# LayerNorm ahead of the MLP: every second eviction of its transposes moved from ScalarE to VectorE

## The chip, the cores and the metric

The kernel runs on one NeuronCore of a Trainium2 chip. The metric is device time in microseconds (us) of one execution; lower is better. A core has TensorE for matmuls and transposes (in the profile PE, its weight loads PEld), VectorE (DVE), ScalarE (ACT), GpSimd (POOL) and SyncE (SP); each works through its own list of instructions in order. TensorE writes only to PSUM, in banks of 128 partitions by 512 float32; VectorE and ScalarE read results from there ("evict" them) into SBUF.

## The reference

A decoder trunk of two layers, in float32, on 1024 tokens of width 1024. Each layer is a token mixer of four head groups, an output projection with a residual and a LayerNorm, and an MLP with a squared ReLU, again with a residual and a LayerNorm:

```python
mix = jnp.concatenate([y_a, y_b, y_c, y_d], axis=-1) @ w_out[l]
h = layer_norm(DEEPNORM_ALPHA * h + mix, ln1_g[l], ln1_b[l])
ff = jnp.square(jax.nn.relu(h @ w_up[l])) @ w_down[l]
h = layer_norm(DEEPNORM_ALPHA * h + ff, ln2_g[l], ln2_b[l])
```

`layer_norm` subtracts the mean of a row, divides by the standard deviation, multiplies by g and adds b. `w_up` is 1024 by 4096 and `w_down` 4096 by 1024.

## The kernel before

**Matmuls.** Every float32 matmul is made of three with operands split in a high and a low part (`mm3`, lines 247 to 249, and `mm3_on`, line 256). Splitting costs a copy on ScalarE (the high part) and a subtraction on VectorE (the low part): for weights in `split_w` (lines 217 and 218), for activations in `to_act` (lines 210 and 211), for the MLP's hidden values in `prep` (lines 1186 and 996).

**The stage around the change.** The output projection adds its results to eight token tiles `z` of 128 tokens by 1024 (line 954: VectorE adds a PSUM bank `pg`). After every second tile, `ln_stats` (lines 139 to 150) gives mean and reciprocal deviation of two tiles, ScalarE writes the normalised tiles `zu` (line 962), and `to_act` turns them into the MLP's operand with channels on partitions. For a pair of token tiles it takes the 8 blocks of 128 channels two at a time, `j` = 0 and 1: one PSUM tile `pt` of 512 columns holds both, each filled by two transposes (line 202). A block is then evicted with g and b of its channels as scale and offset (line 207 on ScalarE, or line 204 on VectorE), into the float32 tile `f`, which is kept for the MLP (`keep`); two blocks together are split into `mh` (ScalarE, line 210) and `ml` (VectorE, line 211). Per layer that is 4 pairs of 4 `pt` tiles, so 64 transposes, 32 evictions and 16 splits. Only this call of `to_act` passes `keep`; the calls for the first LayerNorm and for the last one of a layer do not. `pt` has two buffers (`NPT`), `zu` shares the 13 buffers of `z`, where three are left for it.

VectorE also turns each `z` into the residual for the MLP (lines 1307 and 1308), 1024 columns at a time, once the tile's `zu` exists. TensorE goes on with the first quarter of the MLP's first product (`up_plain`; `pg` from `mh`, `ml` and the split weights `wuh`, `wul`), which ScalarE evicts with ReLU and square (lines 1019 and 1020). From the second quarter on the MLP runs as a Strassen product with 7 in place of 8 block products (`up_steps`, `down_steps`). It needs sums of the quarters of the activations: `sums_of_input` (line 1030) makes them from the `f` tiles on VectorE (`f` by lines 996 and 999), splits them (`sx`, lines 1038 on ScalarE and 996 on VectorE) and has GpSimd write them to DRAM (`sd`, line 1041), from where `fetch` reads them later (`s`, line 1055). Meanwhile the first `down_steps` prepares its operands (`sa`, `wd`) on the same two engines.

**What sets the order.** The program is recorded in the order of the Python code and then put in order for each engine by a scheduler that simulates a time line (`schedule_with_timeline_sim=True`), with `boost()` raising the priority of some pieces. At run time each engine keeps that order and waits where an operand is not there. In the names below the pairs of token tiles have these `pt` tiles in the first layer: pt_5571, 5582, 5591, 5602 (first pair), 5684, 5693, 5702, 5711 (second), 5793, 5804, 5813, 5824 (third), 5906, 5915, 5924, 5933 (fourth); f00 and f01 (f_5254, f_5255) belong to the first four token tiles, f10 and f11 to the others, and so do the `mh` and `ml` of these numbers.

Of the kernel before, what the change touches and what calls it, by code (L numbers as in the profile page):

```python
# [44 lines left out]
def trunk_kernel(ctx, tc, x, ln_in_g, ln_in_b, w_in, conv_w, conv_b, rg_wa, rg_ba, rg_wx, rg_bx, rg_lambda,  # L45
# [29 lines left out]
    def t_u(dt, shape, nm):  # L75
        return big.tile(shape, dt, tag="u", name=nm, bufs=4)

    def t_m(shape, nm):
        return mid.tile(shape, F32, tag="m", name=nm, bufs=NM)
# [10 lines left out]
    def p_t():  # L90
        return pm.tile([P, 512], F32, tag="t", name="pt", bufs=NPT)
# [95 lines left out]
    def to_act(act, zs, nt, gcol, bcol, keep=None):  # L187


        half, o, n = nt // 4, (nt % 4) * P, len(zs)  # L190
        kn = 4 // n
        for g in range(KT // kn):
            pt = p_t().rearrange("p (k c) -> p k c", k=kn)
            k0 = kn * g
            if keep is None:
                h32 = t_m([P, kn, n * P], "h32")
            else:
                h32 = keep[half][k0 // 4][:, k0 % 4:k0 % 4 + kn, o:o + n * P]
            for j in range(kn):
                k = k0 + j  # L200
                for i in range(n):
                    T.transpose(pt[:, j, i * P:(i + 1) * P], zs[i][:, k * P:(k + 1) * P], ident)
                if n == 1 and j % 2:
                    V.tensor_scalar(out=h32[:, j, :], in0=pt[:, j, :], scalar1=gcol[:, k:k + 1],
                                    scalar2=bcol[:, k:k + 1], op0=ALU.mult, op1=ALU.add)
                else:
                    A.activation(h32[:, j, :], pt[:, j, :], AF.Identity, scale=gcol[:, k:k + 1], bias=bcol[:, k:k + 1])
            hi, lo = act.alloc(half, k0 // 4)
            hs, ls = [t[:, k0 % 4:k0 % 4 + kn, o:o + n * P] for t in (hi, lo)]
            A.activation(hs, h32, AF.Copy)  # L210
            V.tensor_tensor(out=ls, in0=h32, in1=hs.bitcast(F32), op=ALU.subtract)
# [633 lines left out]
    for n0, n1 in FIRST:  # L845
        zp = zs[n0:n1]
        ln_unit(zp)
        to_act(act, zp, n0, *ln_in)
        for i in range(n0, n1):
            nc.sync.dma_start(out=spill[i], in_=zs[i])  # L850
        if n0 >= AHEAD:
            next(first, None)
# [19 lines left out]
    for l in range(DEPTH):  # L872
# [72 lines left out]
        keep = [[t_u(F32, [P, 4, 512], f"f{h}{g}") for g in range(2)] for h in range(2)]  # L945
        wo.append(load_out(1))
        for n in range(2):
            for nt in range(NT):
                t = slice((nt % 4) * P, (nt % 4) * P + P)
                ps = p_g()  # L950
                mm3(ps, [((ya.get(0, 2 * j + k, nt // 4)[:, t], ya.get(1, 2 * j + k, nt // 4)[:, t]),
                          (wo[n][j][0][k], wo[n][j][1][k])) for j in KOUT for k in range(2)])
                zc = zs[nt][:, 512 * n:512 * n + 512]
                V.tensor_tensor(out=zc, in0=zc, in1=ps, op=ALU.add)  # L954
                if n == 1 and nt % 2:
                    pair = slice(nt - 1, nt + 1)
                    mean, r = ln_stats(zs[pair], mv[:, pair, :], rs[:, pair])
                    nb = t_s([P, 2], "lnnb")
                    V.scalar_tensor_tensor(out=nb, in0=mean, scalar=-1.0, in1=r, op0=ALU.mult, op1=ALU.mult)
                    zu = [t_z([P, DM], "zu") for _ in range(2)]  # L960
                    for i in range(2):
                        A.activation(zu[i], zs[nt - 1 + i], AF.Identity, scale=r[:, i:i + 1], bias=nb[:, i:i + 1])
                    to_act(act, zu, nt - 1, *[c[:, 8 * l:8 * l + 8] for c in ln1], keep)
# [305 lines left out]
        def last_down(c, us):  # L1269
# [15 lines left out]
            for nt in range(NT):  # L1285
                t = slice(nt * P, nt * P + P)
                for n in range(2):
                    ps = p_g()
                    o = slice(n * 512, n * 512 + 512)
                    mm3(ps, [((us[i][0][:, f, t], us[i][1][:, f, t]), (ws[2 * i + f][0][:, o], ws[2 * i + f][1][:, o]))  # L1290
                             for i in range(2) for f in range(2)])
                    zc = zs[nt][:, o]
                    with boost() if nxt is None and nt == NT - 1 else nullcontext():
                        V.tensor_tensor(out=zc, in0=zc, in1=ps, op=ALU.add)
                if nxt is None:
                    with boost() if nt == NT - 1 else nullcontext():
                        ln_full(zs[nt], gb, bb, out[0, nt * P:(nt + 1) * P, :], nt == NT - 1)
                elif nt % 2:
                    zp = zs[nt - 1:nt + 1]
                    ln_unit(zp)  # L1300
                    to_act(nxt, zp, nt - 1, *[c[:, 8 * l:8 * l + 8] for c in ln2])
                    for i in range(2):
                        nc.sync.dma_start(out=spill[nt - 1 + i], in_=zp[i])
# [95 lines left out]
```

## Time and profile before

| | |
|---|---|
| runs shown | 2425.48, 2427.72, 2433.21 us; median 2427.72 us |
| the profiled execution | 2428.56 us, its span 2426.8 us |
| TensorE busy | 2362.7 us, 97% of the span |
| VectorE busy | 1759.9 us, 73% |
| ScalarE busy | 1115.3 us, 46% |
| granted TensorE clock, mean | 0.994 |
| mean DMA rate | 99 GB/s |

Shares of the whole span say little about a stage. The views used below are the windows (busy time of each engine in a stretch, with the granted TensorE clock), the list of who waited for whom, the groups of like instructions with their mean duration, and the time line of one engine, where a bracket at a row's end gives the idle time before it and what ended that. Matmuls are pipelined: the duration of one is longer than the distance to the next.

### The profile page before, as it was taken

The numbers are of one execution on the slowest core, as the hardware profiler recorded it, in microseconds if no ns is written. First come the engines' busy times: TensorE is split into PE (matmuls) and PEld (weight loads), VectorE is DVE, ScalarE is ACT, GpSimd is POOL, SyncE is SP. The second block draws the span as 40 slices with busy tenths as digits, with TensorE's granted clock in tenths as the row PEclk, the third lists the DMA queues.
The fourth block names the chain that finished last, engine by engine and source line by source line (L and its number), as shares of the span: only waits on it lengthen the run. The fifth ranks groups of instructions, "written<-read, shape, count | busy, mean of one in ns | idle before, by whom it ended". The sixth has DMA issues, their size and how long they took to land.

```text
span 2426.8 us, 35032 instructions
## 1 busy us (share of the span) xinstructions
PE 2362.7 (97%) x13924; PEld 1966.9 (81%) x13924; DVE 1759.9 (73%) x3088; ACT 1115.3 (46%) x1737; POOL 99.4 (4%) x180
## 2 busy tenths in 40 slices
PE   7999999999899999999999999999998999999997
PEld 6888888877788888888798887888777888888886
DVE  6467785766977787777745758856669777787778
ACT  6424655526444345444462346482264444345441
POOL 0000011000100000000000000300001000000000
PEclk9999999999999999999999999999999999999999
DMA  5211133220833224322221011512126433224322
GB/s 198 58 36 45 36 111 111 87 87 18 312 122 111 98 87 139 122 90 95 85 86 46 28 36 40 194 57 87 53 85 244 139 122 106 102 87 139 122 70 87
DMA packets 126971, 241.31 MB, mean 99 GB/s; under 512 B 8924, under 2 KB 81240, under 8 KB 118616
## 3 DMA queue, kind: packets, MB, share of 16 engines
q1 hardware_dynamic: 106032, 135.55, 17.1%
q0 software_dynamic: 19648, 102.80, 11.7%
q8 instruction: 110, 1.80, 0.3%
q10 hardware_dynamic: 1128, 0.72, 0.1%
q14 instruction: 53, 0.43, 0.1%
HBM read 201.29 MB, written 37.75 MB: 99 GB/s over the span
## 4 chain that ended last, share of the span: by engine, by line
PE 67%; issue 21%; DVE 8%; ACT 1%; DMA 1%; POOL 1%; DVEq 0%; POOLq 0%; ACTq 0%
PE pg L256 19%; PE pt L256 11%; PE pg L248 7%; PE pg L247 7%; PE pg L249 7%; PE ps L256 5%; PE po L256 3%; PE po L600 2%; PE pt L592 2%; DVE wdl L218 2%; DVE z L999 1%; PE ps L407 1%; DVE wd L996 1%; PE ps L413 1%; DVE s L999 1%
## 5 line engine op out<-in xcount | busy, mean ns | idle before, releaser
L218 DVE TENSOR_TENSOR wul<-wu,wuh 128x1024 fp32r<-128x1024 f32 x106 | 129.4, 1220 | 130.9 <-PE pg L256 55.1
L256 PE MATMUL pg<-wdh,sa 128*128 128x512 f32 x560 | 184.9, 396 | 6.0 <-DVE z L999 6.0
L217 ACT ACTIVATE wuh<-wu 128x1024 fp32r<-128x1024 f32 x106 | 111.8, 1056 | 123.3 <-PE po L256 54.5
L218 DVE TENSOR_TENSOR wdl<-wd,wdh 128x1024 fp32r<-128x1024 f32 x96 | 117.0, 1219 | 43.8 <-ACT wdh L217 26.9
L256 PE MATMUL pt<-s,wuh 128*128 128x512 f32 x448 | 137.9, 389 | 0.0
L256 PE MATMUL pg<-s,wuh 128*128 128x512 f32 x448 | 137.9, 389 | 0.0
L256 PEld LDWEIGHTS pg<-wdh,sa 128*128 128x128 f32 x560 | 107.1, 191 | 30.2 <-DVE z L999 6.9
L256 PE MATMUL pt<-wdh,sa 128*128 128x512 f32 x352 | 117.2, 393 | 7.0 <-DVE sa L996 4.5
L217 ACT ACTIVATE wdh<-wd 128x1024 fp32r<-128x1024 f32 x96 | 101.0, 1053 | 41.5 <-PE pg L256 12.8
L996 DVE TENSOR_TENSOR sa<-u,sa 128x512 fp32r<-128x512 f32 x140 | 91.4, 682 | 38.7 <-ACT sa L1186 38.7
L256 PE MATMUL ps<-wdh,sa 128*128 128x512 f32 x352 | 116.3, 390 | 0.0
L256 PE MATMUL pg<-mh,wuh 128*128 128x512 f32 x280 | 108.9, 389 | 0.0
L256 PE MATMUL pg<-ml,wuh 128*128 128x512 f32 x280 | 108.9, 389 | 0.0
L256 PE MATMUL pg<-wdl,sa 128*128 128x512 f32 x280 | 108.7, 396 | 0.0
L256 PE MATMUL pg<-mh,wul 128*128 128x512 f32 x280 | 108.6, 389 | 0.0
L247 PE MATMUL pg<-wo,yh 128*128 128x512 f32 x256 | 102.8, 402 | 3.1 <-DVE z L954 2.7
L248 PE MATMUL pg<-wo,yh 128*128 128x512 f32 x256 | 102.0, 398 | 0.0
L249 PE MATMUL pg<-wo,yl 128*128 128x512 f32 x256 | 99.9, 397 | 0.0
L256 PEld LDWEIGHTS pg<-s,wuh 128*128 128x128 f32 x448 | 84.1, 188 | 17.4
L256 PEld LDWEIGHTS pt<-s,wuh 128*128 128x128 f32 x448 | 84.1, 188 | 17.4
L1186 ACT ACTIVATE sa<-u 128x512 fp32r<-128x512 f32 x140 | 82.2, 623 | 22.7 <-PE ps L256 10.0
L999 DVE TENSOR_TENSOR z<-z,pg 128x512 f32<-128x512 f32 x140 | 90.2, 677 | 0.0
(411 smaller groups left out, 6872.0 us busy)
## 6 DMA issues: line engine op xcount, KB each, us to landing
s<-sd POOLq DMA_DIRECT2D x64, 1024.0 KB, 7.3
wu<-in_w_up_dram SPq DMA_DIRECT2D x64, 512.0 KB, 3.7
wd<-in_w_down_dram SPq DMA_DIRECT2D x64, 512.0 KB, 3.6
sd<-sx POOLq DMA_DIRECT2D x32, 512.0 KB, 7.9
spill<-z SPq DMA_DIRECT2D x16, 512.0 KB, 4.4
wb<-in_w_in_dram SPq DMA_DIRECT2D x16, 512.0 KB, 4.3
rs<-spill POOLq DMA_DIRECT2D x32, 256.0 KB, 5.9
resid<-rs POOLq DMA_DIRECT2D x32, 256.0 KB, 4.9
```

Of the source, the lines that this page charges most:

```text
L217: A.activation(hi, raw, AF.Copy)
L218: V.tensor_tensor(out=lo, in0=raw, in1=hi.bitcast(F32), op=ALU.subtract)
L247: T.matmul(ps, ah, bh, start=(i == 0), stop=False)
L248: T.matmul(ps, ah, bl, start=False, stop=False)
L249: T.matmul(ps, al, bh, start=False, stop=(i == n - 1))
L256: T.matmul(ps, a, b, start=(first and i == 0 and j == 0), stop=(i == n - 1 and j == 2), skip_group_check=not first)
L407: T.matmul(ps[r, c, :], k[r, cs], q[r, cs], start=True, stop=True)
L592: T.transpose(pt[:, j * P:(j + 1) * P], s[:, j * P:(j + 1) * P], ident)
L600: T.matmul(po[DH * par:DH * par + DH, (nb % 4) * P:(nb % 4 + 1) * P], vt[:, kb, e:e + DH], wts[par][:, j * P:(j + 1) * P], start=(diag and ...
L996: V.tensor_tensor(out=out, in0=x, in1=y, op=ALU.subtract)
L999: V.tensor_tensor(out=out, in0=x, in1=y, op=ALU.add)
L1186: A.activation(hi, src, AF.Copy)
```

## The change

The condition that chooses VectorE for the odd one of two blocks held only where one token tile is handled alone (`n == 1`); now it holds also where `keep` is given, that is in the LayerNorm ahead of the MLP, in both layers.

```diff
-                if n == 1 and j % 2:
+                if j % 2 and (n == 1 or keep is not None):
                     V.tensor_scalar(out=h32[:, j, :], in0=pt[:, j, :], scalar1=gcol[:, k:k + 1],
                                     scalar2=bcol[:, k:k + 1], op0=ALU.mult, op1=ALU.add)
                 else:
                     A.activation(h32[:, j, :], pt[:, j, :], AF.Identity, scale=gcol[:, k:k + 1], bias=bcol[:, k:k + 1])
```

Per layer 16 of 32 evictions move. The scheduler answers by another order on every engine, from the first pair's evictions to the first steps of `down_steps`; before and behind these stretches the order is the same. Three places in the first layer matter below; the second layer has the same order under other numbers.

**First place, VectorE, the second pair of token tiles.** Before, these rows stand between the last additions of the output projection:

```order
L218 TENSOR_TENSOR wul_6027<-wu_6024,wuh_6026 128x1024
L1308 SCALAR_TENSOR_TENSOR z_5240<-z_5240,rs_77,lnp_5250 128x1024
L218 TENSOR_TENSOR wul_6033<-wu_6030,wuh_6032 128x1024
L140 BN_AGGR mv_76<-lnst_5885 128x2
L954 TENSOR_TENSOR z_5246<-z_5246,pg_5859 128x512
L211 TENSOR_TENSOR ml00_5579<-f00_5254,mh00_5578 128x2x256 x2
```

Now:

```order
L218 TENSOR_TENSOR wul_6027<-wu_6024,wuh_6026 128x1024
L1308 SCALAR_TENSOR_TENSOR z_5240<-z_5240,rs_77,lnp_5250 128x1024
L218 TENSOR_TENSOR wul_6033<-wu_6030,wuh_6032 128x1024
L954 TENSOR_TENSOR z_5246<-z_5246,pg_5859 128x512
L140 BN_AGGR mv_76<-lnst_5885 128x2
L204 TENSOR_SCALAR f00_5254<-pt_5684,lnc1_850 128x256
L204 TENSOR_SCALAR f00_5254<-pt_5693,lnc1_850 128x256
L139 BN_STATS lnst_5885<-z_5246 128x6
L211 TENSOR_TENSOR ml00_5579<-f00_5254,mh00_5578 128x2x256
```

The evictions of pt_5684 and pt_5693 stand on VectorE behind the weight splits, the residual and the last addition.

**Second place, TensorE, between the third and the fourth pair.** Before:

```order
L202 MATMUL pt_5906<-ident_91,zu_5902 128x128
L247 MATMUL pg_6063<-mh01_5598,wuh_6032 128x512
L248 MATMUL pg_6063<-ml01_5599,wuh_6032 128x512
L249 MATMUL pg_6063<-mh01_5598,wul_6033 128x512
L247 MATMUL pg_6063<-mh01_5598,wuh_6032 128x512
L248 MATMUL pg_6063<-ml01_5599,wuh_6032 128x512
L249 MATMUL pg_6063<-mh01_5598,wul_6033 128x512
L247 MATMUL pg_6063<-mh01_5598,wuh_6032 128x512
L248 MATMUL pg_6063<-ml01_5599,wuh_6032 128x512
L249 MATMUL pg_6063<-mh01_5598,wul_6033 128x512
L202 MATMUL pt_5906<-ident_91,zu_5903 128x128
```

Now:

```order
L249 MATMUL pg_6063<-mh01_5598,wul_6033 128x512
L202 MATMUL pt_5813<-ident_91,zu_5789 128x128
L202 MATMUL pt_5813<-ident_91,zu_5790 128x128
L202 MATMUL pt_5824<-ident_91,zu_5789 128x128
L202 MATMUL pt_5824<-ident_91,zu_5790 128x128
L202 MATMUL pt_5906<-ident_91,zu_5902 128x128
L202 MATMUL pt_5915<-ident_91,zu_5902 128x128
L202 MATMUL pt_5906<-ident_91,zu_5903 128x128
L202 MATMUL pt_5915<-ident_91,zu_5903 128x128
```

The last transposes of the third pair and the first of the fourth stand back to back, 16 transposes in a row up to the next matmul, which reads mh10; no matmul is left between them.

**Third place, the end of the LayerNorm.** The first sum of the input (line 999) on VectorE, before and then now:

```order
L211 TENSOR_TENSOR ml10_5801<-f10_5256,mh10_5800 128x2x256 x2
L211 TENSOR_TENSOR ml11_5821<-f11_5257,mh11_5820 128x2x256
L999 TENSOR_TENSOR f11_5257<-f10_5256,f11_5257 128x1024
L996 TENSOR_TENSOR f10_5256<-f00_5254,f10_5256 128x1024
L996 TENSOR_TENSOR sx1_6216<-f11_5257,sx0_6215 128x1024
L211 TENSOR_TENSOR ml11_5821<-f11_5257,mh11_5820 128x2x256
```

```order
L211 TENSOR_TENSOR ml10_5801<-f10_5256,mh10_5800 128x2x256 x2
L204 TENSOR_SCALAR f11_5257<-pt_5924,lnc1_850 128x256
L204 TENSOR_SCALAR f11_5257<-pt_5933,lnc1_850 128x256
L211 TENSOR_TENSOR ml11_5821<-f11_5257,mh11_5820 128x2x256 x2
L999 TENSOR_TENSOR f11_5257<-f10_5256,f11_5257 128x1024 x2
```

The first sum stands behind the evictions of pt_5924 and pt_5933. Before, the second halves of their transposes were apart on TensorE: those of pt_5924 stood three matmuls behind the first halves, those of pt_5933 twenty-one. Now all stand twenty matmuls behind:

```order
L247 MATMUL pg_6144<-mh10_5800,wuh_6026 128x512
L248 MATMUL pg_6144<-ml10_5801,wuh_6026 128x512
L249 MATMUL pg_6144<-mh10_5800,wul_6027 128x512
L202 MATMUL pt_5924<-ident_91,zu_5902 128x128
L202 MATMUL pt_5924<-ident_91,zu_5903 128x128
L202 MATMUL pt_5933<-ident_91,zu_5902 128x128
L202 MATMUL pt_5933<-ident_91,zu_5903 128x128
```

On ScalarE the sums' high parts (sx0, line 1038) move behind evictions of the MLP's first product: before, four of them stand ahead of `u10_5954<-pg_6090` (line 1019), now one.

## Rows read from the trace of the kernel before

**Rows 1.** The page: busy times of each engine; the chain that ended last.

```profile
PE 2362.7 (97%) x13924; PEld 1966.9 (81%) x13924; DVE 1759.9 (73%) x3088; ACT 1115.3 (46%) x1737; POOL 99.4 (4%) x180
...
PE 67%; issue 21%; DVE 8%; ACT 1%; DMA 1%; POOL 1%; DVEq 0%; POOLq 0%; ACTq 0%
```

**Rows 2.** Windows: stretch, length, busy time of each engine (instructions), TensorE clock, DMA.

```profile
571.00:577.00 6.00, 4.32 (x22) 2.53 (x21) 6.00 (x9) 5.67 (x11) 0.00 (x0) 1.00 0.51 165
577.00:599.00 22.00, 22.00 (x106) 17.93 (x105) 10.54 (x19) 13.02 (x22) 0.00 (x0) 1.00 0.01 4
599.00:604.00 5.00, 3.53 (x19) 2.09 (x18) 1.91 (x3) 4.62 (x10) 0.00 (x0) 1.00 0.00 0
...
644.00:649.00 5.00, 5.00 (x15) 3.92 (x16) 5.00 (x7) 2.04 (x3) 0.66 (x2) 0.66 1.11 403
```

**Rows 3.** Waits of TensorE from 540 to 660: us in total, times, longest.

```profile
PE pt L256 <- DVE sa L996: 2.9, 1, 2.9
PE pt L202 <- ACT f L207: 2.3, 4, 0.8
PE pg L256 <- DVE z L999: 2.2, 1, 2.2
```

**Rows 4.** Groups by line and shape, whole run: count | busy us, mean ns | idle before.

```profile
L207 ACT ACTIVATE f<-pt,lnc 128x256 f32<-128x256 f32 x64 | 34.2, 565 | 34.7 <-PE pt L202 34.7
...
L954 DVE TENSOR_TENSOR z<-z,pg 128x512 f32<-128x512 f32 x32 | 21.7, 682 | 23.5 <-PE pg L249 23.1
```

**Rows 5.** The same groups, of VectorE alone: its small reads of PSUM.

```profile
L672 DVE TENSOR_TENSOR bsc<-ps,decay 128x256 f32<-128x256 f32 x32 | 12.7, 418 | 3.1 <-PE ps L671 2.9
...
L204 DVE TENSOR_SCALAR h<-pt,lnc 128x128 f32<-128x128 f32 x8 | 3.1, 398 | 0.0
```

**Rows 6.** Time line of VectorE around the second pair: start, length, instruction, idle before.

```profile
562.11 1.28 DVE L139 BATCH_NORM_STATS2 lnst<-z 128x6 f32<-128x512 f32 x2
564.58 1.28 DVE L1307 SCALAR_TENSOR_TENSOR z<-z,mv,lnp 128x1024 f32<-128x1024 f32 x1 [1.19 <-ACT zu L962]
...
574.71 1.29 DVE L211 TENSOR_TENSOR ml<-f,mh 128x512 fp32r<-128x512 f32 x2
```

**Rows 7.** Time line of TensorE around the second pair.

```profile
570.92 0.60 PE L202 MATMUL pt<-ident,zu 128*128 128x128 f32 x4
571.95 0.89 PE L202 MATMUL pt<-ident,zu 128*128 128x128 f32 x4 [0.44 <-ACT f L207]
```

**Rows 8.** Time line of ScalarE around the fourth pair.

```profile
595.70 1.25 ACT L962 ACTIVATE zu<-z,lnnb,rs 128x1024 f32<-128x1024 f32 x1 [0.90 <-PE pt L202]
...
600.77 0.64 ACT L1020 ACTIVATE u<-u 128x512 f32<-128x512 f32 x1
...
602.19 0.65 ACT L210 ACTIVATE mh<-f 128x512 fp32r<-128x512 f32 x1
```

**Rows 9.** Time line of TensorE around the fourth pair.

```profile
599.18 0.49 PE L202 MATMUL pt<-ident,zu 128*128 128x128 f32 x3
600.48 0.89 PE L202 MATMUL pt<-ident,zu 128*128 128x128 f32 x4 [0.82 <-ACT f L207]
...
602.89 0.96 PE L247 MATMUL pg<-mh,wuh 128*128 128x512 f32 x3
```

**Rows 10.** Time line of VectorE: first sum of the input, longest wait, first addition into z.

```profile
606.14 1.22 DVE L999 TENSOR_TENSOR f<-f,f 128x1024 f32<-128x1024 f32 x1
...
621.07 1.22 DVE L996 TENSOR_TENSOR sx<-f,sx 128x1024 fp32r<-128x1024 f32 x1 [3.85 <-DMA sd<-sx]
...
643.18 1.87 DVE L999 TENSOR_TENSOR z<-z,pg 128x512 f32<-128x512 f32 x3
```

**Rows 11.** Time line of TensorE: release by that addition, and the second layer's counterparts.

```profile
643.90 0.50 PE L256 MATMUL pg<-wdh,sa 128*128 128x512 f32 x1 [2.22 <-DVE z L999]
...
1798.41 0.90 PE L202 MATMUL pt<-ident,zu 128*128 128x128 f32 x4 [0.81 <-ACT f L207]
...
1840.62 0.79 PE L256 MATMUL pg<-wdh,sa 128*128 128x512 f32 x1 [3.81 <-DVE z L999]
```

## The prediction

> **What bounds the kernel now.** TensorE is busy for 97% of the span and holds 67% of the chain that ended last [rows 1]; VectorE has slack on average. So an edit costs what it adds to TensorE's waits. I read the windows next, 4 us at a time: in the stage that changes TensorE is full except from 571 to 577, from 599 to 604 [rows 2] and in a third stretch ahead of 644. The list of waits names the causes [rows 3]: in the first two stretches it waits for ScalarE's evictions `f` (2.3 us in all), in the third for VectorE, for `sa` (2.9) and for an addition into `z` (2.2). VectorE, which is to get more work, ends the last and longest waits. [...]
>
> **Prices.** ScalarE loses 32 evictions at 0.565 us [rows 4], 9.0 us per layer. VectorE gains 32. Its nearest rows are an eviction by the same line of half the columns, 0.398, and a read of PSUM of the same 128x256, 0.418 [rows 5]; an upper bound is the 512 columns of line 954, 0.682 [rows 4]. I take 0.50, nearer to the same width than to the double one, and 0.45 from one to the next, since starts follow faster than durations: 8.0 us per layer. Were it 0.40, each of about four evictions that lie on the path of a layer would give back 0.1 us, 0.8 us in all; at 0.68 they cost 1.5 us more. [...]
>
> What matters is not the price but the queue. ScalarE stood ready when transposes ended: it idled 34.7 us ahead of these evictions, waiting for TensorE [rows 4]. VectorE has other work ahead of its share. And the split is by `j`, the halves of one `pt` tile: ScalarE takes the first half of both tiles, VectorE the second half of both. The engines do not work side by side; TensorE waits first for one, then for the other.
>
> **First place (second pair).** VectorE is in step with before until the two statistics at 562.11 [rows 6]. Now two evictions follow (563.3 to 564.2), which fill most of the old wait of 1.19 for `zu`; then the same ten instructions as before, from 564.58 to 574.71 then, 10.1 us, without a gap. So VectorE comes to the evictions of pt_5684 and pt_5693 at 574.4. TensorE has their transposes done at 571.5, 0.44 before it went on last time [rows 7], and its next transposes need those two buffers: it waits until 574.9 for the first, 575.4 for the second. That is a wait of about 3.5 us in one piece where 0.44 was. The small ones that followed (0.48 and 0.65) go. After a short wait for `ml` the second halves of pt_5702 start at 577.3.
>
> From there to the third pair's last transposes are 106 instructions of TensorE, 16 of them transposes. The window from 577 to 599 holds 106 too, with 15 transposes, in 22.00 us, all busy [rows 2]; VectorE and ScalarE have room there (10.5 and 13.0 of 22). I take 22.1: 599.4.
>
> **Second place (fourth pair).** Sixteen transposes in a row now wait for one engine after the other. Those of the third pair end at 599.9. The two evictions on VectorE let pt_5906 and pt_5915 start at 600.6 and 601.1, with zu_5902. zu_5903 needs the buffer of zu_5789, which is read until 599.9; before, it ran from 595.70 with nine matmuls in front of its use [rows 8], now its 1.25 us lie bare, behind an activation, and it is there at 601.6. ScalarE then has an activation and two `mh` ahead of the first halves' evictions, at some 0.52 each from start to start (durations 0.64 and 0.65 [rows 8]): the evictions end at 603.6 and 604.1, and the second halves' transposes at 604.3. VectorE has meanwhile lines 1307 and 1308 and two `ml` (3.6 us from 601.7) and evicts from 605.3. The next first halves run to 606.4, the matmul behind them at 606.45. Before, it stood at 602.89 [rows 9]; the same instructions lie ahead of it. TensorE is 3.6 us late, both places together, at full clock.
>
> **Third place (sums of the input).** VectorE needs pt_5924 and pt_5933 complete, twenty matmuls on: 4.5 us at the pace of that full window, so 611.2. Two evictions and two `ml` later the first sum starts at 613.7; before 606.14 [rows 10], 7.6 us later. From there to the first addition into `z` took 37.04 us, of which 3.85 were a wait for a DMA buffer [rows 10]. Now one `ml` less (0.60) is in between, and the DMA wait should go, since the writes start later; against that some 0.8 for ScalarE's `sx` halves, which stand behind MLP evictions. That is 33.4 us, so 647.1 in place of 643.18: 3.9 us. This addition releases TensorE (643.90) [rows 11], and behind it the order is the old one, so the delay stays. In the second layer, 1197.93 us later by the transposes at 600.48 [rows 9] and 1798.41, the release came at 1840.62 [rows 11], 1.2 us sooner than the first layer's shifted one; the same walk makes it 5.1 us later. Sum 9.0 us.
>
> **Clock.** Two new long waits per layer, 3.5 us in one piece and about 5 us idle of 7 in the second place, resemble the one ahead of 644 and not the 2.5 us in pieces ahead of 577 or 604, behind which the clock stayed at 1.00 [rows 2]. I price each at the 1.7 us of rows 2: 6.8 us. The waits at the sums keep their drop, already in the time of before.
>
> Sum: 9.0 + 6.8 = 15.8 us on the execution's own 2428.56, 2444.4; the median of the runs lies 0.84 below that execution, so I predict **2443 us**.
>
> **Rivals.**
> 1. *The waits come, the clock stays up.* The idle time of the second place is broken by transposes. Then only 9.0 us: 2437. This differs from the forecast by the clock rows alone.
> 2. *Hidden.* VectorE's sums take up the delay: the DMA wait of 3.85 and TensorE's own 2.9 + 2.2 [rows 3] are slack if the MLP's operands are ready as early as before. Against it: these waits are for VectorE itself, which then has no idle time to give back. Time 2428, give or take 3.
> 3. *Faster.* If VectorE comes to each eviction within half a microsecond, the two engines clear the banks faster than one, the 2.3 us of waits for `f` go [rows 3], and with VectorE's sums started sooner one clock drop of 1.7 [rows 2] per layer: 2 x 4.0, 2420. It decides at 574.4: were VectorE there by 572, this would be the likeliest. Against it stand the ten instructions ahead of it [rows 6]. [...]
> 4. *It does not do what it says* is excluded: the order of the instructions shows 16 evictions on VectorE per layer.
>
> **How the numbers follow.** Forecast 50%, first rival 25%, second 15%, third 10%. About 0.3% (7.3 us) is what a measurement of this kernel can tell from no change. The forecast is nearly always above it; the first rival, at 9.0 with an uncertainty of 3, in two cases of three; the second nearly never; the third is faster by over 0.3% in six of ten. That gives slower 0.69, same 0.25, faster 0.06. The range runs from the first rival less its uncertainty and the price of an eviction at 0.40, 2431, to the forecast with the higher price and the DMA wait still there in both layers (1.5 + 7.7), 2452.
>
> **What would show it.** Right: a wait of TensorE of 3 us or more for `f` on VectorE (line 204) near 572, its matmul behind the sixteen transposes near 606 to 608, a first sum (line 999) at 613 or later, ScalarE's idle time ahead of line 207 smaller, clock below 1.00 near 576 and 607. Wrong: a start of the first sum by 608, or waits of TensorE for VectorE's `f` under 2 us per layer; then VectorE was free earlier than its list of work says. If the first sum starts late and the release near 644 does not move, the second rival holds.

## The result, and the profile after

The changed kernel takes 2445.07 us (median of 4 runs, 2442.36 to 2448.93) against 2427.43 (4 runs, 2425.48 to 2433.21): ratio 1.0074, 95% interval 1.0061 to 1.0088. It is slower by about 18 us. The profiled execution took 2448.93 us, its span 2447.2.

The page, busy times and the chain that ended last (answers to [rows 1]):

```profile
PE 2372.3 (97%) x13924; PEld 1976.0 (81%) x13924; DVE 1774.8 (73%) x3120; ACT 1098.6 (45%) x1705; POOL 99.4 (4%) x180
...
PE 80%; DVE 9%; issue 4%; ACT 4%; DMA 2%; POOL 0%; SPq 0%; DVEq 0%; POOLq 0%; ACTq 0%
```

VectorE has 32 instructions and 14.9 us more, ScalarE 32 and 16.7 us fewer, as the change says. VectorE's share of the span is 73% as before, and still the kernel is slower. The waits of TensorE from 540 to 670 us (answers to [rows 3]):

```profile
PE pg L256 <- DVE z L999: 5.4, 1, 5.4
PE pt L202 <- DVE f L204: 5.1, 3, 3.4
PE pt L202 <- ACT f L207: 1.6, 1, 1.6
```

Three waits of 5.1 us for the new evictions, one of them 3.4 long, and the wait for the addition into `z` has grown from 2.2 to 5.4, while the wait of 2.9 for `sa` has shrunk to 0.3. The groups (answers to [rows 4, 5]):

```profile
L207 ACT ACTIVATE f<-pt,lnc 128x256 f32<-128x256 f32 x32 | 16.2, 557 | 25.8 <-PE pt L202 25.8
L204 DVE TENSOR_SCALAR f<-pt,lnc 128x256 f32<-128x256 f32 x32 | 16.0, 536 | 36.6 <-PE pt L202 36.6
```

An eviction on VectorE lasts 0.536 us, hardly less than one on ScalarE. VectorE idled 36.6 us ahead of its 32, waiting for TensorE: most of them find VectorE ready.

**Where the time is.** The two executions are not in step even ahead of the change: the two statistics that stood at 562.11 [rows 6] stand at 566.80, 4.69 us later. Only the first evictions of the first pair are new ahead of them, and these need not be the cause: in the profiles of the kernels below that move nothing ahead of them, they stand anywhere from 561.68 to 567.21. Times in the profile after are therefore read less 4.69. VectorE and TensorE at the first place:

```profile
566.80 1.28 DVE L139 BATCH_NORM_STATS2 lnst<-z 128x6 f32<-128x512 f32 x2
567.99 0.98 DVE L204 TENSOR_SCALAR f<-pt,lnc 128x256 f32<-128x256 f32 x2
...
579.05 0.94 DVE L204 TENSOR_SCALAR f<-pt,lnc 128x256 f32<-128x256 f32 x2
```

```profile
579.60 1.14 PE L202 MATMUL pt<-ident,zu 128*128 128x128 f32 x4 [3.44 <-DVE f L204]
...
1785.46 1.14 PE L202 MATMUL pt<-ident,zu 128*128 128x128 f32 x4 [3.44 <-DVE f L204]
```

VectorE comes to the second pair's first evictions at 579.05, that is 574.36 on the clock of before. TensorE has waited 3.44 for them, in both layers alike. From layer to layer the transposes now stand 1205.86 apart; before it was 1197.93 [rows 9, 11]: 7.93 us more from one to the other. So the 20.4 us between the two spans are 4.69 ahead of the change, 7.93 from the first layer's stage on and, as what remains, 7.8 from the second's.

TensorE at the second place, the sixteen transposes in a row and the matmul behind them (before 602.89 [rows 9]):

```profile
605.38 0.60 PE L202 MATMUL pt<-ident,zu 128*128 128x128 f32 x4
606.47 1.32 PE L202 MATMUL pt<-ident,zu 128*128 128x128 f32 x4 [0.49 <-DVE f L204]
609.37 0.98 PE L202 MATMUL pt<-ident,zu 128*128 128x128 f32 x4 [1.57 <-ACT f L207]
611.53 1.14 PE L202 MATMUL pt<-ident,zu 128*128 128x128 f32 x4 [1.19 <-DVE f L204]
612.33 1.63 PE L247 MATMUL pg<-mh,wuh 128*128 128x512 f32 x3
```

The waits go VectorE, ScalarE, VectorE: each group of transposes waits for the evictions of one engine (they start at 605.87 on VectorE, 608.76 on ScalarE and 610.94 on VectorE), while the other has none of its own to do. VectorE at the third place, and the release of TensorE:

```profile
622.05 2.35 DVE L999 TENSOR_TENSOR f<-f,f 128x1024 f32<-128x1024 f32 x2
...
631.62 1.23 DVE L996 TENSOR_TENSOR sx<-f,sx 128x1024 fp32r<-128x1024 f32 x1 [0.21 <-ACT sx L1038]
...
654.73 1.89 DVE L999 TENSOR_TENSOR z<-z,pg 128x512 f32<-128x512 f32 x3
```

```profile
655.48 0.80 PE L256 MATMUL pg<-wdh,sa 128*128 128x512 f32 x1 [5.43 <-DVE z L999]
```

The first sum is 11.2 us late (617.36 for 606.14 [rows 10]). By the first addition into `z` it is 6.9 (650.04 for 643.18): the wait of 3.85 for a DMA is gone, only 0.21 for ScalarE is left. The windows behind the three places show the clock (the last number but two), which was 1.00 at the first two before [rows 2]:

```profile
580.00:584.00 4.00, 4.00 (x16) 3.24 (x15) 3.21 (x11) 1.82 (x5) 0.00 (x0) 0.66 0.31 113
608.00:612.00 4.00, 1.43 (x6) 0.71 (x7) 3.93 (x6) 2.25 (x5) 0.00 (x0) 0.76 0.01 2
612.00:616.00 4.00, 4.00 (x13) 3.23 (x12) 1.29 (x2) 1.57 (x4) 0.00 (x0) 0.50 0.00 0
616.00:620.00 4.00, 4.00 (x19) 3.27 (x18) 0.41 (x1) 0.00 (x0) 0.00 (x0) 0.89 0.00 0
656.00:660.00 4.00, 4.00 (x11) 3.05 (x10) 4.00 (x6) 1.69 (x2) 0.00 (x0) 0.50 1.11 419
660.00:664.00 4.00, 4.00 (x17) 3.20 (x16) 4.00 (x8) 1.18 (x2) 1.06 (x2) 0.84 1.12 354
```

The pace of the matmuls goes with the clock: where it reads 1.00 they start 0.230 us apart (603.77 to 605.15), where it reads 0.50, 0.428 (613.75 to 615.89). The losses are estimates from the clock; by these two paces a microsecond at 0.50 loses 0.46. Where TensorE is busy, 4 us at a clock of 0.66 lose 4 x 0.34 = 1.4; the second drop loses 2.0 + 0.4 = 2.4; the third 2.0 + 0.6 = 2.6, which is 0.9 more than the 1.7 of before. In the second layer the third drop went the other way. TensorE's release there, then the clock behind it, before (two windows) and after (two windows):

```profile
1861.48 0.80 PE L256 MATMUL pg<-wdh,sa 128*128 128x512 f32 x1 [5.43 <-DVE z L999]
```

```profile
1840.00:1844.00 4.00, 3.38 (x8) 2.70 (x9) 4.00 (x6) 2.10 (x3) 1.60 (x3) 0.50 1.07 382
1844.00:1848.00 4.00, 4.00 (x13) 3.10 (x13) 4.00 (x7) 1.82 (x3) 0.00 (x0) 0.65 1.10 408
```

```profile
1860.00:1864.00 4.00, 2.52 (x6) 2.03 (x7) 4.00 (x6) 1.42 (x2) 0.54 (x1) 0.50 1.16 369
1864.00:1868.00 4.00, 4.00 (x14) 3.17 (x14) 4.00 (x7) 1.66 (x3) 1.07 (x2) 0.73 1.12 392
```

Where TensorE is busy, it lost 3.38 x 0.50 + 4 x 0.35 = 3.1 before and 2.52 x 0.50 + 4 x 0.27 = 2.3 after.

### The profile page after: what moved, and what is told of

Read it like the earlier page. It is cut to its first block, busy times and chain, and to the rows that moved or that the text cites. A ratio compares the mean times of both kernels' runs of the same rounds, so it can differ in the third digit from the quotient of the medians.

```text
span 2447.2 us, 35056 instructions
## 1 busy us (share of the span) xinstructions
PE 2372.3 (97%) x13924; PEld 1976.0 (81%) x13924; DVE 1774.8 (73%) x3120; ACT 1098.6 (45%) x1705; POOL 99.4 (4%) x180
## 4 chain that ended last, share of the span: by engine, by line
PE 80%; DVE 9%; issue 4%; ACT 4%; DMA 2%; POOL 0%; SPq 0%; DVEq 0%; POOLq 0%; ACTq 0%
PE pg L256 18%; PE pg L247 11%; PE pg L248 11%; PE pg L249 11%; PE pt L256 10%; PE ps L256 4%; PE po L256 3%; PE po L600 2%; PE pt L592 2%; DVE z L999 1%; DVE wdl L218 1%; PE pt L202 1%; PE ps L407 1%; DVE wd L996 1%; ACT wdh L217 1%
```

## The experiments

The theory: VectorE works through its list in order and comes late to a few evictions, at the second pair above all; TensorE waits for it in one piece (3.44 us) and then runs at a lower clock (0.66). The rivals: the load (each moved eviction costs its own time wherever it stands), and the new order of TensorE (sixteen transposes in a row cost, whoever evicts). Each ratio is to the kernel before, run beside it on the same chip. The edits are shown against the changed kernel; the two bases that move no eviction have the condition of the kernel before.

### One pair of token tiles at a time

```diff
-                if j % 2 and (n == 1 or keep is not None):
+                if j % 2 and (n == 1 or (keep is not None and nt == 2)):
```

`nt == 2` is the second pair; 0, 4 and 6 are the first, third and fourth.

> Only the first pair's four odd evictions per layer move to VectorE (tokens 0 to 255); the other three pairs stay on ScalarE. Theory (TensorE waits where VectorE comes late in its own list, price does not matter): VectorE is in step here, two evictions fill its old wait for zu, so TensorE's waits for f stay under 1 us per layer and the time is that of before, 2427, within 2 us. Rival (load: each moved eviction costs its own duration wherever it stands): four of 0.54 us per layer, 2.2, or a quarter of the whole change, some 4 us slower, 2431. Rival (the new order itself): as much slower as the order differs, here almost nothing, so this run cannot tell it.

> Only the second pair's four odd evictions per layer move. Theory: VectorE reaches the first two of them behind the weight splits, the residual and the last addition, at about 574.4 on the clock of before; TensorE waits 3 us or more in one piece for f on VectorE, its clock drops behind, and the sixteen transposes in a row follow; TensorE is some 7 us late at the first sum, of which about 4 us are taken up again by VectorE's wait for the DMA buffer in the sums (3.85 before): 3 us per layer, 6 in all, 2433 (2430 to 2438). Load rival: the same as every other pair, some 4 us, 2431, and no single wait of 3 us. If the second place has a price of its own that the sums do not take up, 10 or more, 2437.

> Only the third pair's four odd evictions per layer move; the order of VectorE is otherwise that of before and TensorE's hardly differs. Theory: VectorE has idle time here (10.5 us of work in 22), so it comes at once; the time is that of before, 2427, within 2 us, or up to 2 us less as the waits for ScalarE at the fourth pair shorten. Load rival: some 4 us slower, 2431.

> Only the fourth pair's four odd evictions per layer move, straight ahead of the sums of the input. Theory: TensorE's transposes keep their places, the first sum comes about 0.5 to 1.5 us later, and the wait for the DMA buffer in the sums takes that up: 2427, within 2 us. Load rival: the four evictions stand on VectorE where it has no idle time up to the release near 643, so 2.2 us per layer, 4.3 in all, 2432.

Measured: first pair 0.9999 (0.9990 to 1.0009), third 0.9999 (0.9990 to 1.0008), fourth 0.9993 (0.9984 to 1.0001); second 1.0056 (1.0041 to 1.0070), 13.6 us. The load falls: four evictions cost nothing that can be told in three places, and in one about three quarters of what the whole change does. My 6 us for the second pair missed; the third case named there, "10 or more", came. TensorE and VectorE of the second pair alone:

```profile
577.89 1.07 PE L202 MATMUL pt<-ident,zu 128*128 128x128 f32 x4 [3.79 <-DVE f L204]
```

```profile
630.51 1.22 DVE L996 TENSOR_TENSOR sx<-f,sx 128x1024 fp32r<-128x1024 f32 x1 [3.19 <-DMA sd<-sx]
```

The wait at the first place is there in full. But the wait for the DMA in the sums, which I expected to take up 4 us of the delay, has moved along and still lasts 3.19. So the delay at the first sum, 6.6 us, arrives whole at the addition into `z`, 6.9 (table below).

That delay is not the long wait alone. The sixteen transposes in a row are here too, and in this run none of the evictions that they wait for stands on VectorE:

```profile
605.30 0.33 PE L202 MATMUL pt<-ident,zu 128*128 128x128 f32 x1 [0.70 <-ACT f L207]
606.42 0.90 PE L202 MATMUL pt<-ident,zu 128*128 128x128 f32 x3 [0.80 <-ACT zu L962]
608.37 0.44 PE L202 MATMUL pt<-ident,zu 128*128 128x128 f32 x2 [1.05 <-ACT f L207]
609.35 1.14 PE L202 MATMUL pt<-ident,zu 128*128 128x128 f32 x4 [0.53 <-ACT f L207]
```

```profile
612.00:616.00 4.00, 4.00 (x11) 3.09 (x11) 2.08 (x3) 1.78 (x4) 0.00 (x0) 0.50 0.00 0
```

These waits are for ScalarE, 3.1 us and a clock of 0.50 behind them. So a part of what the second pair costs falls in the new order of TensorE, with evictions on ScalarE.

### Two evictions per layer, and all but the second pair

```diff
+                if j % 2 and (n == 1 or (keep is not None and nt == 2 and g < 2)):
```

```diff
+                if j % 2 and (n == 1 or (keep is not None and nt != 2)):
```

> Only two evictions per layer move: the second halves of the second pair's first two pt tiles (pt_5684, pt_5693 in the first layer). Theory (VectorE comes to these two late, TensorE waits in one piece, everything behind is moved by that): the wait of 3 us or more is here in full, and the order of TensorE behind it is that of the pair alone, so the time is that of the pair alone within 3 us, 2441 (2437 to 2443). Load rival: half of the pair's cost, 2434.

> Twelve of the sixteen evictions per layer move, all but the second pair's. Theory: VectorE has idle time at each of them; 2427, within 3 us, with 24 evictions moved. Load rival: three quarters of the whole change, 13 us slower, 2440.

Measured: two evictions per layer 1.0044 (1.0031 to 1.0057), some 10 us, at the low end of what I expected and above the load's 2434; the twelve others 1.0005 (0.9996 to 1.0013). Four evictions of the whole kernel make more than half of the loss, twenty-four make none that can be told. The four bring the row of sixteen with them, with the same waits for ScalarE as above (0.71, 0.80, 1.06 and 0.54). The single wait for VectorE:

```profile
574.87 1.14 PE L202 MATMUL pt<-ident,zu 128*128 128x128 f32 x4 [3.78 <-DVE f L204]
```

### Taking away what stands ahead of them: first try, on GpSimd

The low halves of the first up weights go to GpSimd, with the two evictions moved and, as a base, with none.

```diff
-            V.tensor_tensor(out=lo, in0=raw, in1=hi.bitcast(F32), op=ALU.subtract)
+            (nc.gpsimd if nm == "wu" and first else V).tensor_tensor(out=lo, in0=raw, in1=hi.bitcast(F32), op=ALU.subtract)
```

> The two evictions of the second pair move, and the weight splits that stand ahead of them in VectorE's list (two of 1.2 us) are on GpSimd. Theory: VectorE comes 2.4 us sooner, TensorE's wait of 3.8 for f on VectorE falls to about 1.4, and its clock drops less behind it; 2.4 to 4.1 us per layer come back, so 5 to 8 us below the run with the two evictions alone: 2433 to 2436. Rival (price or order, not the queue): no more than 1 us per layer comes back, 2439 or later.

> No eviction moves: the kernel before, but the four low halves of the first weights of the MLP's first product (wul) are subtracted on GpSimd in place of VectorE. By this the scheduler gives TensorE sixteen transposes in a row between the third and the fourth pair, as the change does, with all evictions on ScalarE. Theory (VectorE's late evictions): no wait of TensorE for f on VectorE; the row of transposes by itself costs at most 2 us per layer: 2428 to 2431. Rival (the scheduler's new order is the cause, wherever the evictions run): most of what the second pair alone costs, 8 us or more, 2436 or later. If GpSimd is slow with the subtractions, TensorE waits for wul instead, which the list of waits would show.

Measured: 1.0084 (1.0071 to 1.0097) and 1.0062 (1.0050 to 1.0074), both against what the theory said of them. VectorE, GpSimd and TensorE of the first of the two:

```profile
573.03 5.03 DVE L211 TENSOR_TENSOR ml<-f,mh 128x512 fp32r<-128x512 f32 x2
...
579.84 0.99 DVE L204 TENSOR_SCALAR f<-pt,lnc 128x256 f32<-128x256 f32 x2
```

```profile
571.85 5.66 POOL L218 TENSOR_TENSOR wul<-wu,wuh 128x1024 fp32r<-128x1024 f32 x2 [43.74 <-ACT wuh L217]
```

```profile
580.43 1.14 PE L202 MATMUL pt<-ident,zu 128*128 128x128 f32 x4 [5.27 <-DVE f L204]
```

The edit did the opposite of what it was made for: while GpSimd subtracts, two subtractions of VectorE take 5.03 us in place of 1.29 [rows 6], and VectorE comes later still (14.08 us behind its two statistics at 565.76, with the two evictions alone 12.60, from 561.68). TensorE's wait follows it one for one: 5.27 in place of 3.78, 1.49 more for 1.48. That supports the mechanism, by the wrong sign. The base without moved evictions has the same trouble at an addition of VectorE, so it does not tell what the row of transposes costs:

```profile
578.90 0.79 PE L247 MATMUL pg<-mh,wuh 128*128 128x512 f32 x1 [2.71 <-DVE z L954]
```

### Taking away what stands ahead of them: second try, the residual left out

```diff
-        for i, z in enumerate(zs):
-            V.scalar_tensor_tensor(out=z, in0=z, scalar=mv[:, i, 0:1], in1=gb, op0=ALU.subtract, op1=ALU.mult)
-            V.scalar_tensor_tensor(out=z, in0=z, scalar=rs[:, i:i + 1], in1=bb, op0=ALU.mult, op1=ALU.add)
         sums_of_input()
```

> All evictions on ScalarE as before; lines 1307 and 1308, the residual of the MLP on VectorE (two of 1.2 us per token tile), are left out, so the second LayerNorm's input lacks the residual's rescaling. It is the base for the next two. TensorE's order now has fourteen transposes in a row between the third and the fourth pair, with no late eviction: theory (VectorE's lateness is the cause): no wait for f above 1.1 us, 2420 to 2429. Rival (the row of transposes is the cause): 5 us or more above before, 2432 or later.

> The same without the residual, with the second pair's first two odd evictions on VectorE (pt_5684, pt_5693). TensorE's order is that of the base. Without the residual 4.8 us of the work ahead of them is gone from VectorE's list. Theory: VectorE is there within a microsecond, TensorE's wait of 3.8 us becomes 1 us or less, and the time is that of the base within 3 us, where it was 10 us more with the residual. Rival (price, or the engine itself): the 10 us stay.

> The same without the residual, with the whole change, sixteen evictions per layer on VectorE. Theory: with VectorE in time everywhere the change costs at most 4 us against the base, and may gain, since two engines clear the banks; the wait for f on VectorE stays under 1.5 us in one piece. Rival (load): 16 of 0.54 us on VectorE per layer keep most of the 17 us.

Measured: 0.9994 (0.9986 to 1.0003), 0.9990 (0.9979 to 1.0001) and 0.9987 (0.9978 to 0.9995). Without the residual the whole change costs nothing that can be told. Its waits of TensorE, then VectorE and TensorE at the first place:

```profile
PE pt L256 <- DVE sa L996: 2.7, 1, 2.7
PE pt L202 <- DVE f L204: 1.9, 3, 0.8
PE pg L256 <- DVE z L999: 1.4, 1, 1.4
```

```profile
571.46 0.99 DVE L204 TENSOR_SCALAR f<-pt,lnc 128x256 f32<-128x256 f32 x2
```

```profile
572.05 0.89 PE L202 MATMUL pt<-ident,zu 128*128 128x128 f32 x4 [0.80 <-DVE f L204]
```

The same sixteen evictions per layer, 0.54 us each, on the same engine: VectorE is at the two in question 9.57 us behind its statistics (561.89) in place of 12.25, the wait is 0.80 in place of 3.44, and the clock stays at 1.00 in all windows of 4 us from 572 to 624. The edit takes more away than the work ahead of the two evictions: VectorE loses the residual of all eight token tiles, and the order of TensorE changes as well. In the base, fourteen transposes stand in a row, with a longest wait of 1.05 for ScalarE, and its time shows that less work on VectorE and this row together change nothing; what each does alone it does not show. With the whole change there are twelve in a row, not sixteen, and then three matmuls:

```profile
599.37 0.78 PE L202 MATMUL pt<-ident,zu 128*128 128x128 f32 x4 [0.71 <-DVE f L204]
600.22 0.96 PE L247 MATMUL pg<-mh,wuh 128*128 128x512 f32 x3
```

So with VectorE in time and a shorter row the loss is gone; which part each has in that is not shown. With the two evictions moved, the clock still fell to 0.61 from 600 to 604, behind the row of transposes, and the addition into `z` came 2.2 us later than in the base, too little to show in the time. What sixteen cost stays open: no run has sixteen in a row with VectorE in time, nor VectorE this late without the row.

### The split by tile

```diff
-                if j % 2 and (n == 1 or keep is not None):
+                if (j % 2 and n == 1) or (keep is not None and g % 2):
```

> The same number of evictions moved, but by pt tile and not by half: VectorE takes both blocks of every second tile (pt_5582, 5602, 5693, 5711 and so on), ScalarE both of the others. Theory: TensorE has ScalarE's bank to go on with while VectorE is late with its own, so the single wait for f on VectorE at the second pair is under 1.5 us in place of 3.4; the row of transposes between the third and fourth pair costs up to 3 us per layer: 2426 to 2434. Rival (load): the same VectorE work as the change, 2443 or later.

Measured: 1.0041 (1.0028 to 1.0054), 10 us: better than the split by halves, outside what I expected. The long wait at the second pair is gone, as expected (no wait there is over 0.66 us); the row of transposes costs more:

```profile
605.02 0.44 PE L202 MATMUL pt<-ident,zu 128*128 128x128 f32 x2 [0.64 <-DVE f L204]
606.22 0.44 PE L202 MATMUL pt<-ident,zu 128*128 128x128 f32 x2 [0.76 <-ACT zu L962]
607.99 1.11 PE L202 MATMUL pt<-ident,zu 128*128 128x128 f32 x4 [1.33 <-DVE f L204]
609.76 0.69 PE L202 MATMUL pt<-ident,zu 128*128 128x128 f32 x2 [0.66 <-ACT f L207]
```

```profile
608.00:612.00 4.00, 3.34 (x10) 2.17 (x11) 3.77 (x6) 2.46 (x5) 0.00 (x0) 0.50 0.00 0
```

3.4 us of waits in one place, the longest again for VectorE, and the clock falls to 0.50 behind them.

### All runs by one measure

Microseconds from the two statistics of VectorE (562.11 in [rows 6]) to its first sum of the input and to its first addition into `z` from `pg`, in the first layer, with TensorE's longest wait for an eviction on VectorE and the ratio. Times are from one profiled execution of each kernel:

| kernel | wait | first sum | first `z` | ratio |
|---|---|---|---|---|
| before | none | 44.03 | 81.07 | 1 |
| the change | 3.44 | 55.25 | 87.93 | 1.0074 |
| first pair alone | none | 44.05 | 79.50 | 0.9999 |
| second pair alone | 3.79 | 50.60 | 87.92 | 1.0056 |
| third pair alone | none | 44.10 | 80.87 | 0.9999 |
| fourth pair alone | 0.3 | 43.77 | 80.64 | 0.9993 |
| its first two evictions | 3.78 | 51.23 | 86.96 | 1.0044 |
| pairs 1, 3 and 4 | 0.26 | 43.73 | 79.99 | 1.0005 |
| two evictions, GpSimd | 5.27 | 55.82 | 88.80 | 1.0084 |
| none moved, GpSimd | none | 53.57 | 86.56 | 1.0062 |
| no residual, none moved | none | 43.00 | 78.55 | 0.9994 |
| no residual, two moved | 0.61 | 43.93 | 80.79 | 0.9990 |
| no residual, the change | 0.80 | 41.61 | 79.08 | 0.9987 |
| by tile | 1.33 | 48.13 | 84.59 | 1.0041 |

Every kernel whose addition into `z` comes 3 us late or more is slower, and no other is. No version here is shown to beat the kernel before.

## Why the prediction was right, point by point

**The price.** 0.50 taken, 0.536 measured. It did not matter, as 24 moved evictions at that price cost nothing.

**First place.** VectorE at 574.4 predicted, 574.36 measured; the wait 3.5, measured 3.44. The cause of the wait is shown: with 4.8 us of the work ahead of the two evictions gone it is 0.80, and where VectorE came 1.48 us later still it was 1.49 longer. That the loss goes with it holds for the runs without the residual, where the order of TensorE differs too.

**Second place.** TensorE 3.6 late at full clock, with the first drop of 1.7 5.3; measured 607.64 less 602.89 = 4.75. The three waits in the row add up to 3.25 us, for VectorE and ScalarE in turn as the walk had them. With the second pair alone moved, a row of the same length waits 3.1 us for ScalarE alone, so the waits of this place are not VectorE's doing alone.

**Third place.** First sum 7.6 late at full clock, with two drops 11.0; measured 11.2. From there to `z` 33.4 predicted, 32.68 measured: the 0.8 for ScalarE's `sx` was 0.21. The wait for the DMA went, but the reason that I gave ("since the writes start later") is wrong: with the second pair alone the writes start later too, and 3.19 of it stay. Why it goes in the change is not settled.

**Clock.** Two drops of 1.7 per layer, which is 5.00 us at 0.66, 5.00 x 0.34 [rows 2]: measured 1.4 and 2.4. "The waits at the sums keep their drop" holds in neither layer alone: 2.6 in place of 1.7 in the first, 2.3 in place of 3.1 in the second. Over both it comes out nearly even, and that is luck. The prediction also overlooked a drop of before: from 632 to 636 in the first layer, behind the waits for `sa`, the clock stood at 0.61, and in the same place after the change (636 to 644) it stays at 1.00. The wait for `z` behind it, which ends with VectorE's addition, can take up what that gives back; no run shows it apart.

**Sum.** 15.8 predicted, 17.6 measured between the medians. In the trace the two stages lose 7.9 and 7.8 us, 15.7 in all, where the walk had 3.9 + 3.4 = 7.3 and 5.1 + 3.4 = 8.5: the release is 6.9 late in the first layer and, by the statistics of its own layer, 8.2 in the second. That the two layers' misses cancel to 0.1 is luck too. The 15.7 is from one execution and the 17.6 from medians of four; no run here explains the 1.9 between them. Two smaller sums do not come out: the low end, put together as described, is 2437 - 3 - 0.8 = 2433 and not 2431, and the chances given for slower add up to about 0.5 + 0.25 x 2/3 = 0.67 and not 0.69.

Every sign named came: a wait of 3 us or more near 572, the matmul behind the row at 607.6, the first sum later than 613, less idle time of ScalarE ahead of line 207 and a lower clock behind the first two places.

The first rival (clock stays up) falls by the clock rows. The second (hidden) named a real effect, 4.4 of 11.2 us are taken up, but not its size. The third was to decide at 574.4: "were VectorE there by 572, this would be the likeliest". The whole change without the residual puts VectorE there (571.68 on the clock of before). The loss goes, as that rival needs, but the gain of 8.0 us that it priced does not come: 0.9987 against 0.9994 of its base, intervals that overlap. Evicting with both engines was worth nothing measurable with VectorE in time, and cost 0.74% with VectorE late.

## What to carry to other kernels

Before moving work to an engine with free time on average, find the row where that engine will come to it: four of the 32 moved evictions here, behind 10 us of other work in VectorE's list, made more than half of the loss, and 24 others nothing that can be told. Look at the order that the scheduler answers with as well: here a row of sixteen transposes came with these four evictions, and it waits even where ScalarE does the evicting (3.1 us with the second pair alone moved). Here the halves of one bank went to two engines, and TensorE got it back when the later of the two was done: ScalarE evicted from 573.69 to 574.71, VectorE from 579.05, and TensorE went on at 579.60. With whole banks in turn no wait at the second pair was over 0.66 us. The wait of 3.44 us on TensorE cost more than its length: behind it the clock fell to 0.66, another 1.4 us.

## What the runs showed that I had not expected

GpSimd's two subtractions of 128x1024 float32 took 5.66 us, 2.83 each, where one of VectorE's takes 1.22, and while they ran VectorE's two subtractions `ml`, 1.29 us together in [rows 6], took 5.03. The statistics that VectorE began in the same stretch (line 139, at 572.42) kept their length, 0.68 us as before:

```profile
572.42 0.68 DVE L139 BATCH_NORM_STATS2 lnst<-z 128x6 f32<-128x512 f32 x1
```

So it is not VectorE as a whole that stood still, but the two subtractions: they lasted from 573.03 to 578.06, GpSimd's from 571.85 to 577.51. In the base without moved evictions the same two took 5.07 us beside 5.69 of GpSimd. What held them up is not shown.

A second thing: the longer list of work did not show in the averages. VectorE stood at 73% busy before and after, and its idle time ahead of the 32 moved evictions (36.6 us) was larger than ScalarE's had been ahead of 64 (34.7 [rows 4]).
